# Two gates and the second modulation as row products on TensorE in four column groups, and one-column steps in VectorE's threshold search, in a decoder layer

## The chip, the cores and the metric

The kernel runs on one core of a Trainium2 chip. A core has five engines that run their own instruction streams and wait for each other by semaphores: TensorE (PE; its weight loads are listed as PEld), VectorE (DVE), ScalarE (ACT), GpSimd (POOL) and SyncE (SP), whose queue here issues nearly all DMA transfers. The metric is the device time of one execution in microseconds; lower is better.

## The reference

One decoder layer on x of 1024 tokens and 1024 channels in f32, conditioned by a vector c:

```
mod = silu(c) @ w_mod + b_mod        # 6 rows: shift1, scale1, gate1, shift2, scale2, gate2
h   = x * (1 + scale1) + shift1
q, k, v, u, iq, ik, iw = split(h @ w_in)
score = sum_h iw_h * relu(rope(iq)_h . rope(ik))      # causal
attn  = softmax attention of 8 heads over the 256 best keys by score
mix   = concat(attn, causal pooling of u over 2, 4, 8, 16 tokens) @ w_o
x = layer_norm(alpha * x + gate1 * mix)
h = x * (1 + scale2) + shift2
x = layer_norm(alpha * x + gate2 * ((silu(h @ w_gate) * (h @ w_up)) @ w_down))
```

Each row of mod is a product of the 1024 entries of silu(c) with a 1024 x 1024 block of w_mod (4 MB). The change concerns four of the six rows: gate1 (row 2), shift2 and scale2 (rows 3 and 4) and gate2 (row 5), in the change's own count rows 0 to 3.

## The kernel before, in words

The work stands in stages. First the first modulation and the index projections (to about 75 us). Then the score loop (to about 178 us): index logits on PE (`lg`), relu on ACT, weighted sums on DVE into `score`, for query tiles 2 to 7 of 128 tokens, with the Q projections (`pj`) between them. Then the projection (to about 374 us): 24 groups of 24 matmuls of 512 columns, eight for u (the pooling channels), eight for k and eight for v; their weights come by `raw_slot` transfers on SP's queue and are split into a rounded part (ACT) and a rest (POOL) in `ws_W`. After two groups of u, DVE adds shifted copies (`ub`), ACT and POOL split the result (`phi`, `plo`), and PE multiplies it with the pooling weights (`po`). Then the attention in head groups g = 3 to 0 (to about 545 us), the output product with w_o, a layer norm and the feed-forward part.

The 256 best keys of a query are found by a threshold search on 16-bit keys. DVE searches tiles 7 and 6 together (`colsD`, two columns, one for each tile) and tile 2 alone (`colsE`); ACT searches 5 and 4 together, and 3. `search_v` takes 31 steps a search: a counting pass over each tile's keys with the candidate as a scalar, and then two small operations that turn the counts `cntc` into the new candidate `cand`. The searches are fillers: a planner puts their steps wherever an engine would wait by its own estimates, and the programs of DVE, ACT and POOL are then fixed in the order in which they were written. An engine runs its instructions in that order.

In the score loop one step of `gate_acc` follows each part: a load of 512 KB and one DVE operation of 128 x 1024 that adds silu(c)[k] times the row block to `modacc`. `gate_fin`, at the projection's group 20, sums the partitions with two ones-matmuls (`gt`) and adds the bias. In the attention, from unit 8 on, `mods` runs two steps a unit: 16 DVE products with row sums over 128 x 1024 (`modraw`) for shift2 and scale2, and eight operations on `gacc` for gate2, which goes to `g2_d` by two more `gt`.

## Time and profile before

| | us |
|---|---|
| runs | 1322.65, 1324.58, 1326.92 (median 1324.58) |
| span of the profiled execution | 1321.4, mean granted TensorE clock 0.957 of full speed |
| own time of the profiled execution | not listed beside its span |
| busy in the span | PE 1199.6, PEld 934.3, DVE 1066.3, ACT 648.6, POOL 736.7 |

The profile shows one execution. Busy times of engines overlap, and a share over the whole span is a mean over stages with different limits, so the stages are read apart. The time outside the span (the 3.2 us between it and the median) is taken as it is.

### The profile page before, as it was taken

What the parts mean: (1) busy time and instruction counts of PE and PEld (TensorE: products, weight loads), DVE (VectorE), ACT (ScalarE), POOL (GpSimd) and SP (SyncE); (2) the same over time, 40 slices, a digit from 0 to 9 for tenths busy, and PEclk for the clock granted to TensorE, in tenths of its full rate; (3) what the DMA queues carried; (4) which work ended last, traced back from release to release, by engine and by line L of the source; (5) the groups of instructions that cost most, each with busy time, mean ns of one, the idle gap of its engine ahead of it and who ended that gap; (6) DMA issues with size and microseconds to landing.
All of it is one profiled execution on the core that took longest, in us unless ns stands there. A gap on an engine that the chain in (4) does not pass through costs nothing.

```text
span 1321.4 us, 16106 instructions
## 1 busy us (share of the span) xinstructions
PE 1199.6 (91%) x5462; PEld 934.3 (71%) x5462; DVE 1066.3 (81%) x1828; ACT 648.6 (49%) x1335; POOL 736.7 (56%) x509
## 2 busy tenths in 40 slices
PE   8979895797988996999789999999999999999996
PEld 6646564575855654787677787878788887878775
DVE  6899999999978797477697787776878777777698
ACT  3346673675998776445534243333333333333531
POOL 1392373666213355427678384664848475576848
PEclk8999898798979998999799999999999999999998
DMA  9540020131100266420020101102010111113112
GB/s 343 222 158 29 16 72 24 64 96 42 47 16 9 73 215 239 144 72 9 32 96 32 65 32 64 64 32 96 33 64 32 65 43 53 68 44 112 47 58 119
DMA packets 34904, 103.91 MB, mean 79 GB/s; under 512 B 3843, under 2 KB 3843, under 8 KB 33286
## 3 DMA queue, kind: packets, MB, share of 16 engines
q1 hardware_dynamic: 34822, 102.88, 22.1%
q8 instruction: 43, 0.70, 0.2%
q14 instruction: 39, 0.32, 0.1%
HBM read 93.42 MB, written 9.45 MB: 78 GB/s over the span
## 4 chain that ended last, share of the span: by engine, by line
PE 38%; DVE 6%; POOL 4%; issue 2%; ACT 1%; DVEq 0%; POOLq 0%; ACTq 0%
PE gu L169 24%; PE dn L169 14%; DVE act_W L169 2%; POOL wraw_R L169 1%; DVE utmp_X L169 1%; POOL wraw_W L169 1%; DVE gtmp_V L169 1%; POOL wblk_T L169 0%; DVE wblk_T L169 0%; DVE hr_H L169 0%; POOL hr_H L169 0%; DVE res_X L169 0%; DVE stat_C L169 0%; POOL wblk_V L169 0%; DVE wblk_V L169 0%
## 5 line engine op out<-in xcount | busy, mean ns | idle before, releaser
L169 PE MATMUL gu<-hr_H,wblk_T 128*128 128x512 f32 (+1 forms) x924 | 217.3, 387 | 3.0 <-POOL wblk_T L169 1.9
L169 PE MATMUL gu<-hr_H,wblk_V 128*128 128x512 f32 (+1 forms) x924 | 215.2, 384 | 3.7 <-POOL wblk_V L169 1.9
L169 PEld LDWEIGHTS gu<-hr_H,wblk_T 128*128 128x128 f32 x924 | 172.3, 191 | 39.2 <-POOL wblk_T L169 3.6
L169 PEld LDWEIGHTS gu<-hr_H,wblk_V 128*128 128x128 f32 x924 | 170.0, 188 | 40.1 <-POOL wblk_V L169 3.6
L169 DVE TENSOR_TENSOR res_X<-res_X,dn 128x512 f32<-128x512 f32 (+1 forms) x253 | 159.0, 678 | 15.4 <-PE dn L169 15.3
L169 POOL TENSOR_SCALAR sm_H<-sm_H,stat_X 128x1024 f32<-128x1024 f32 (+7 forms) x64 | 58.6, 928 | 124.1 <-DVE stat_X L169 112.5
L169 PE MATMUL pj<-ws_W,hT_H 128*128 128x512 f32 x456 | 119.4, 409 | 4.4 <-ACT pout_K L169 2.0
L169 POOL TENSOR_TENSOR wraw_R<-wraw_R 128x512 f32<-128x512 f32 x64 | 94.5, 1484 | 46.9 <-DVE wblk_T L169 23.7
L169 POOL TENSOR_TENSOR wraw_W<-wraw_W 128x512 f32<-128x512 f32 x60 | 86.7, 1452 | 58.0 <-DVE wblk_V L169 29.3
L169 PEld LDWEIGHTS pj<-ws_W,hT_H 128*128 128x128 f32 x456 | 85.1, 192 | 30.0 <-issue 10.1
L169 PE MATMUL dn<-wblk_T,act_W 128*128 128x512 f32 x324 | 79.6, 394 | 4.4 <-DVE act_W L169 4.4
L169 PE MATMUL dn<-wblk_V,act_W 128*128 128x512 f32 x324 | 78.5, 391 | 2.9 <-DVE act_W L169 2.5
L169 DVE TENSOR_SCALAR_CACHE_REDUCE junk_X<-keysD_T,colsD_X 128x1024 int16<-128x1024 int16 (+1 forms) x64 | 78.9, 1269 | 0.7
L169 ACT ACTIVATE wblk_V<-wraw_R 128x512 fp32r<-128x512 f32 x56 | 35.2, 629 | 80.7 <-POOL wraw_R L169 62.3
L169 PEld LDWEIGHTS dn<-wblk_T,act_W 128*128 128x128 f32 x324 | 60.9, 189 | 19.1 <-DVE act_W L169 6.5
L169 PEld LDWEIGHTS dn<-wblk_V,act_W 128*128 128x128 f32 x324 | 60.4, 188 | 17.4 <-DVE act_W L169 4.2
L169 POOL TENSOR_TENSOR ws_W<-raw_R,ws_W 128x1024 fp32r<-128x1024 f32 x17 | 44.8, 2652 | 48.6 <-ACT ws_W L169 48.5
L169 ACT ACTIVATE wblk_V<-wraw_W 128x512 fp32r<-128x512 f32 x53 | 33.1, 627 | 75.0 <-POOL wraw_W L169 56.4
L169 ACT ACTIVATE wblk_T<-wraw_W 128x512 fp32r<-128x512 f32 x56 | 35.0, 628 | 66.3 <-POOL wraw_W L169 50.2
L169 ACT ACTIVATE wblk_T<-wraw_R 128x512 fp32r<-128x512 f32 x52 | 32.5, 627 | 60.9 <-POOL wraw_R L169 45.5
L169 ACT ACTIVATE junkA_T<-keys_T,colsA_X 128x768 bf16<-128x768 uint16 (+3 forms) x62 | 54.1, 873 | 9.0 <-DVE colsA_X L169 8.7
L169 ACT ACTIVATE utmp_X<-gu 128x512 f32<-128x512 f32 x33 | 19.7, 598 | 73.4 <-PE gu L169 73.4
(300 smaller groups left out, 2828.1 us busy)
## 6 DMA issues: line engine op xcount, KB each, us to landing
wm_K<-in_wma_dram SPq DMA_DIRECT2D x16, 512.0 KB, 9.5
modraw_V<-in_wmc_dram SPq DMA_DIRECT2D x16, 512.0 KB, 4.5
wraw_R<-in_wg_dram SPq DMA_DIRECT2D x6, 1024.0 KB, 4.9
wraw_R<-in_wd_dram SPq DMA_DIRECT2D x12, 512.0 KB, 3.5
wraw_W<-in_wup_dram SPq DMA_DIRECT2D x12, 512.0 KB, 3.5
modraw_V<-in_wmg_dram SPq DMA_DIRECT2D x10, 512.0 KB, 4.3
wraw_R<-in_wup_dram SPq DMA_DIRECT2D x10, 512.0 KB, 3.5
wraw_W<-in_wg_dram SPq DMA_DIRECT2D x5, 1024.0 KB, 4.9
```

The costliest lines, as they stand in the source:

```text
L169: ins_ = f(*a, **k)
```

## The change

Both gates and the second modulation become row products on PE. The weights of the four rows come as 16 sets of 1 MB (`mset`, three slots in region K, where the score loop's operands were). A half (`mod_half`) is four plain-f32 matmuls with 32 columns of `silb` (32 copies of silu(c)[k]) stationary and 512 columns of the set moving; the four write to the four 32-partition groups of one PSUM bank `md`. Two halves make 512 columns of a row. ACT copies the bank with a scale of 1/32 (`macc`), and a ones-matmul sums the 128 partitions: for the gates as one full-width matmul (`gt`) with a 1 x 512 addition on DVE and a write to `gate_d`, for shift2 and scale2 as four products of one column (`mc`) with an addition of 128 x 4. This is done at the projection's groups 1 to 9, two halves a group. `gate_acc`, `gate_fin` and `mods` go away. The loads go through SP's queue, between the weight loads and behind the writes that stand there.

In `search_v` the two small operations on nt columns become nt operations of one column each, and the second is a TENSOR_SCALAR with the old candidate as a scalar operand, in place of a SCALAR_TENSOR_TENSOR with two tensor inputs.

```diff
@@ -45,7 +45,7 @@
-MODS = (8, 2)
+MOD_AT = 1
...
@@ -302,8 +304,6 @@
     srow = buf("X", 4224, 1024, "srow")
     SP.dma_start(srow, crow_in.to_broadcast([P, 1024]))
     A.activation(srow, srow, AF.Silu)
-    s_d = tc.dram_tile([1, 1024], F32, name="s_d")
-    SP.dma_start(s_d, srow[0:1, :])
@@ -427,93 +427,7 @@
...
-    def gate_acc(row, acc, ring, ahead):
...
-    def mods():
...
+    gate_d = [tc.dram_tile([1, 1024], F32, name=f"gate{q}_d") for q in range(2)]
...
@@ -680,9 +594,11 @@
                     dt = U16 if low else I16
                     V.tensor_scalar(trash(i).bitcast(dt), kv[i].bitcast(dt), one(cand, m), one(base, m),
                                     ALU.is_ge, ALU.add, accum_out=one(cntc, m))
-                V.tensor_scalar(pr, cntc, 0.0, float(1 << b), ALU.is_ge, ALU.mult)
                 off = -float(1 << (b - 1)) if b > 0 else -1.0
-                V.scalar_tensor_tensor(cand, pr, off, cand, ALU.add, ALU.add)
+                for m in range(nt):
+                    V.tensor_scalar(one(pr, m), one(cntc, m), 0.0, float(1 << b), ALU.is_ge, ALU.mult)
+                for m in range(nt):
+                    V.tensor_scalar(one(cand, m), one(pr, m), one(cand, m), off, ALU.add, ALU.add)
 
         def search_a(bits, low):
 
@@ -811,7 +727,6 @@
...
-            next(gate_steps, None)
...
@@ -893,13 +808,52 @@
     def v_take(t, pp):
         A.activation(vst[t // 4][:, t % 4], v3(pp), AF.Copy)
 
-    def gate_fin(dst, acc, row, base):
-        SP.dma_start(base, bg_in[row : row + 1, :].to_broadcast([P, 1024]))
-        for c in range(2):
+    MSET = [buf("K", 2048 + i * 2048, 2048, "mset") for i in range(3)]
+    silb = buf("X", 5312, 256, "silb")
+    grow = buf("X", 5568, 512, "grow")
+    macc = [buf("V", 5616 + i * 512, 512, "macc") for i in range(2)]
+    m_ps = {}
+
+    def mod_load(h):
+
+        if h < 16:
+            SP.dma_start(MSET[h % 3], wmr_in[h // 4, h // 2 % 2, h % 2])
+
+    def mod_half(h):
+
+        s_, part = divmod(h, 2)
+        if part == 0:
+            m_ps[s_] = psA("md")
+        for q in range(4):
+            k = 4 * part + q
+            T.matmul(m_ps[s_][32 * q : 32 * q + 32, :], silb[:, k * 32 : (k + 1) * 32], MSET[h % 3][:, q * 512 : (q + 1) * 512],
+                     start=(part == 0), stop=(part == 1))
+        mod_load(h + 3)
+        if part == 1:
+            A.activation(macc[s_ % 2], m_ps.pop(s_), AF.Copy, scale=1.0 / 32)
+
+    def mod_fin(s_):
+
+        row, c = divmod(s_, 2)
+        acc = macc[s_ % 2]
+        if row in (0, 3):
             pm = psA("gt")
-            cc = slice(c * 512, (c + 1) * 512)
-            T.matmul(pm, ones, acc[:, cc], start=True, stop=True)
-            V.tensor_tensor(dst[:, cc], base[:, cc], pm, ALU.add)
+            T.matmul(pm, ones, acc, start=True, stop=True)
+            V.tensor_tensor(grow[0:1, :], grow[0:1, :], pm[0:1, :], ALU.add)
+            SP.dma_start(gate_d[row // 3][:, c * 512 : (c + 1) * 512], grow[0:1, :])
+            if s_ != 7:
+                n = {0: 1, 1: 6, 6: 7}[s_]
+                SP.dma_start(grow[0:1, :], bg_in[n // 6 : n // 6 + 1, n % 2 * 512 : n % 2 * 512 + 512])
+        else:
+            pc = psA("mc")
+            for j in range(4):
+                T.matmul(pc[:, j : j + 1], acc[:, j * P : (j + 1) * P], ones[:, 0:1], start=True, stop=True)
+            u = (row - 1) * 8 + c * 4
+            V.tensor_tensor(m2[:, u : u + 4], pc[:, 0:4], bcol[:, 16 + u : 20 + u], ALU.add)
+            if s_ == 5:
+                V.scalar_tensor_tensor(h2c[:, 0:8], m2[:, 8:16], 1.0, lnc[:, 0:8], ALU.add, ALU.mult)
+                V.scalar_tensor_tensor(h2c[:, 8:16], m2[:, 8:16], 1.0, lnc[:, 8:16], ALU.add, ALU.mult)
+                V.tensor_tensor(h2c[:, 8:16], h2c[:, 8:16], m2[:, 0:8], ALU.add)
 
     def w_loads(w_in):
         for kp in range(3):
@@ -922,6 +876,11 @@
     while qt[2] or qt[0] < NT:
         q_piece()
     w_loads(wu_in)
+    for h in range(3):
+        mod_load(h)
+    SP.dma_start(lnc, lncol_in)
+    SP.dma_start(grow[0:1, :], bg_in[0:1, 0:512])
+    V.tensor_copy(silb.rearrange("p (k r) -> p k r", r=32), silc.unsqueeze(2).to_broadcast([P, 8, 32]))
     for i in range(4):
         G.memset(ub[i][:, 0:16], 0.0)
     for kp in range(4):
@@ -979,9 +938,17 @@
         else:
             at_(nd, lambda a=a, pp=pp: v_take(a, pp))
         if n_ == 20:
-            at_(n_, lambda: gate_fin(GR, macc, 0, raw_slot()))
+            SP.dma_start(GR, gate_d[0].to_broadcast([P, 1024]))
+        q_ = n_ - MOD_AT
+        if 0 <= q_ < 9:
+            if q_:
+                mod_fin(q_ - 1)
+            if q_ < 8:
+                mod_half(2 * q_)
         for f in late.pop(n_, []):
             f()
+        if 0 <= q_ < 8:
+            mod_half(2 * q_ + 1)
     last = len(groups)
     pinned.clear()
 
@@ -1151,11 +1118,6 @@
                     nrm += 1
             elif step == "T":
                 u_trans(u)
-        if n_ == MODS[0]:
-            mod_steps = mods()
-        if n_ >= MODS[0]:
-            for _ in range(MODS[1]):
-                next(mod_steps, None)
         if g > 0 and (pr, i % 2) in Q_AT:
             t = 2 * (g - 1) + 1 - Q_AT.index((pr, i % 2))
             q_make(t, q_load(t))
@@ -1168,8 +1130,6 @@
     while streams:
         advance(streams[0])
     times.fill = None
-    for _ in mod_steps:
-        pass
     wo_split(1)
     pair_cat(0, 3, pair_pv(0, 3))
     wo_split(2)
...
@@ -1861,8 +1821,7 @@
         "cnt": f(np.broadcast_to(cnt.reshape(1, 64), (P, 64))),
         "crow": f(a["c"][0].reshape(1, D)),
         "wma": f(np.stack([wmt[1], wmt[0]], axis=2).reshape(8, P, 2048)),
-        "wmc": f(wmt[3:5]),
-        "wmg": f(np.stack([wmod[:, :, 2], wmod[:, :, 5]]).reshape(2, 8, P, 1024)),
+        "wmr": f(np.stack([wmod[:, :, r] for r in (2, 3, 4, 5)]).reshape(4, 2, 4, P, 2, 512).transpose(0, 4, 1, 3, 2, 5).reshape(4, 2, 2, P, 2048)),
         "bcol": f(np.concatenate([np.stack([bmod[1].T, bmod[0].T], axis=2).reshape(P, 16), bmod[3].T, bmod[4].T], axis=1)),
         "bg": f(np.stack([bmod[2].reshape(-1), bmod[5].reshape(-1)])),
```

DVE's program, before, around the first `ub` addition of the projection (colsE is tile 2's search, colsD that of tiles 7 and 6):

```order
L169 TENSOR_SCALAR junk_X_614,colsE_X_616<-keysA_X_605,colsE_X_616 128x384
L169 TENSOR_SCALAR colsE_X_616<-colsE_X_616 128x1
L169 SCALAR_TENSOR_TENSOR colsE_X_616<-colsE_X_616 128x1
L169 TENSOR_SCALAR junk_X_614,colsE_X_616<-keysA_X_605,colsE_X_616 128x384
L169 SCALAR_TENSOR_TENSOR ub_V_1234<-ub_V_1234,ub_V_1232 128x1024
L169 TENSOR_SCALAR junk_X_607,colsD_X_615<-keysD_T_609,colsD_X_615 128x1024
```

The same place after (grow is the gate's row, gt its summed product):

```order
L171 TENSOR_TENSOR grow_X_1225<-grow_X_1225,gt_1435 1x512
L171 TENSOR_SCALAR junk_X_601,colsD_X_609<-keysD_T_603,colsD_X_609 128x1024
L171 TENSOR_SCALAR junk_X_602,colsD_X_609<-keysD_T_603,colsD_X_609 128x896
L171 TENSOR_SCALAR colsD_X_609<-colsD_X_609 128x1 x4
L171 TENSOR_SCALAR junk_X_601,colsD_X_609<-keysD_T_603,colsD_X_609 128x1024
L171 TENSOR_SCALAR junk_X_602,colsD_X_609<-keysD_T_603,colsD_X_609 128x896
L171 TENSOR_SCALAR colsD_X_609<-colsD_X_609 128x1 x4
L171 TENSOR_TENSOR grow_X_1225<-grow_X_1225,gt_1505 1x512
L171 SCALAR_TENSOR_TENSOR ub_V_1212<-ub_V_1212,ub_V_1210 128x1024
```

Tile 2's search stands wholly ahead of `ub` now (28 of its 31 steps did before, and 6 steps of colsD where 7 do now), and two gate additions stand ahead of it too.

PE's program, before, at the end of the fourth single u group and the first pooling product:

```order
L169 MATMUL pj_1519<-hT_H_67,ws_W_72 128x512 x3
L169 MATMUL pj_1519<-hT_H_68,ws_W_72 128x512 x3
L169 MATMUL po_1544<-phi_V_1236,wps_X_1231 128x512 x2
L169 MATMUL po_1544<-plo_V_1237,wps_X_1231 128x512
```

PE's program after, from the third row product to the next group (md_1522's second row needs the sixth set):

```order
L171 MATMUL pj_1480<-hT_H_68,ws_W_72 128x512 x3
L171 MATMUL gt_1505<-macc_V_1227,const_C_78 128x512
L171 MATMUL md_1522<-mset_K_1222,silb_X_1224 32x512 x4
L171 MATMUL md_1522<-mset_K_1223,silb_X_1224 32x512 x4
L171 MATMUL pj_1556<-hT_H_61,ws_W_69 128x512 x3
```

Two more groups, two more md pairs and the `mc` of each stand between this and the first `po`, which was the next thing behind the u groups before.

SP's queue, before, from the last piece of wu (in_wu) on:

```order
L166 DMA q_d<-rope_V_454 128x512 x5
L166 DMA raw_R_75<-in_wu_dram 128x1024
L166 DMA raw_R_73<-in_wpool_dram 128x512
L166 DMA raw_R_74<-in_wk_dram 128x1024
L166 DMA raw_R_75<-in_wk_dram 128x1024
L166 DMA q_d<-rope_V_454 128x512
```

SP's queue after, from the same place:

```order
L168 DMA q_d<-rope_V_450 128x512 x5
L168 DMA mset_K_1221<-in_wmr_dram 128x2048
L168 DMA q_d<-rope_V_450 128x512
L168 DMA mset_K_1222<-in_wmr_dram 128x2048
L168 DMA mset_K_1223<-in_wmr_dram 128x2048
L168 DMA raw_R_75<-in_wu_dram 128x1024
...
L168 DMA mset_K_1221<-in_wmr_dram 128x2048
L168 DMA q_d<-rope_V_450 128x512
L168 DMA mset_K_1222<-in_wmr_dram 128x2048
L168 DMA gate_d<-grow_X_1225 1x512
L168 DMA mset_K_1223<-in_wmr_dram 128x2048
```

Three sets stand ahead of the last piece of wu, and the sixth set stands behind the gate's first write, which waits for DVE.

## Rows read from the trace of the kernel before

**Rows 1.** Busy time of each engine in stretches of the span (us, with the number of instructions), then the granted TensorE clock as a share of full speed, the DMA engines' busy share and what they moved: score loop, projection, and three parts of the attention.

```profile
74.00:178.00 104.00, 92.25 (x357) 58.40 (x357) 100.42 (x162) 66.29 (x116) 49.91 (x34) 0.92 0.12 44
178.00:374.00 196.00, 156.46 (x649) 124.20 (x647) 189.43 (x360) 129.92 (x346) 101.88 (x65) 0.90 0.18 59
374.00:442.00 68.00, 60.27 (x311) 37.44 (x312) 45.88 (x94) 60.25 (x143) 19.77 (x18) 0.87 0.04 14
442.00:516.00 74.00, 62.14 (x384) 38.92 (x383) 67.68 (x155) 49.04 (x116) 35.95 (x32) 0.95 0.57 196
516.00:545.00 29.00, 27.79 (x173) 19.31 (x172) 15.94 (x56) 20.72 (x60) 14.56 (x19) 1.00 0.44 155
```

**Rows 2.** What PE waited for in the projection (178 to 374 us): us in total, times, the longest.

```profile
PE po L169 <- ACT ub_V L169: 15.1, 1, 15.1
PE pair L169 <- POOL ws_W L169: 12.2, 4, 4.3
PE kT L169 <- DVE kr_K L169: 5.1, 2, 4.8
PE po L169 <- POOL plo_V L169: 2.5, 2, 1.7
PE pj L169 <- ACT pout_K L169: 2.0, 1, 2.0
PE po L169 <- ACT phi_V L169: 1.3, 1, 1.3
```

**Rows 3.** The timeline (start, duration, instruction; in brackets the idle time before it and its releaser): PE at the end of the score loop and at the first group, PE and DVE at the first pooling product, DVE and PE at the start of the attention.

```profile
171.83 7.09 PE L169 MATMUL pj<-ws_W,hT_H 128*128 128x512 f32 x30
181.26 0.98 PE L169 MATMUL pair<-hT_H,ws_W 128*128 128x512 f32 x3 [1.88 <-POOL ws_W L169]
...
211.81 1.97 PE L169 MATMUL pj<-hT_H,ws_W 128*128 128x512 f32 x8
226.03 1.22 DVE L169 SCALAR_TENSOR_TENSOR ub_V<-ub_V,ub_V 128x1024 f32<-128x1024 f32 x1
228.88 1.22 PE L169 MATMUL po<-phi_V,wps_X 128*128 128x512 f32 x2 [15.09 <-ACT ub_V L169]
...
373.17 0.63 DVE L169 TENSOR_SCALAR score_X<-junk_X 128x896 f32<-128x896 bf16 x1
374.46 0.73 PE L169 MATMUL s<-kr_K,qab_H 128*128 128x512 f32 x2 [1.90 <-ACT qab_H L169]
```

**Rows 4.** DVE's instructions that the change takes away: the first gate in the score loop (groups of one tile, busy us and mean ns behind the bar; the first with its least, median and greatest ns), the second modulation and gate in the attention, and the second gate's additions.

```profile
L169 DVE TENSOR_SCALAR modacc_X<-modraw_T,const_C x1: 1774/1774/1774, 75.6 to 75.6; 128x1024 f32<-128x1024 f32 x1
L169 DVE SCALAR_TENSOR_TENSOR modacc_X<-modraw_T,const_C,modacc_X 128x1024 f32<-128x1024 f32 x3 | 5.9, 1956 | 0.0
L169 DVE SCALAR_TENSOR_TENSOR modacc_X<-modraw_V,const_C,modacc_X 128x1024 f32<-128x1024 f32 x2 | 3.6, 1787 | 0.0
L169 DVE SCALAR_TENSOR_TENSOR modacc_X<-modraw_X,const_C,modacc_X 128x1024 f32<-128x1024 f32 x2 | 3.4, 1698 | 0.0
...
L169 DVE CUSTOM_DVE_ANT_0 modraw_V<-modraw_V,srow_V 128x1024 f32<-128x1024 f32 x16 | 20.3, 1266 | 0.6 <-DMA modraw_V<-in_wmc_dram 0.6
L169 DVE SCALAR_TENSOR_TENSOR gacc_V<-modraw_V,const_C,gacc_V 128x1024 f32<-128x1024 f32 x7 | 10.0, 1431 | 0.0
L169 DVE TENSOR_SCALAR gacc_V<-modraw_V,const_C x1: 740/740/740, 494.2 to 494.2; 128x1024 f32<-128x1024 f32 x1
L169 DVE TENSOR_TENSOR grow_V<-grow_V,gt x2: 670/673/676, 513.7 to 515.4; 1x512 f32<-1x512 f32 x2
```

**Rows 5.** The search's small operations on DVE, 74 to 375 us: busy us and mean ns behind the bar.

```profile
L169 DVE SCALAR_TENSOR_TENSOR colsD_X<-colsD_X 128x2 f32<-128x2 f32 x31 | 18.4, 592 | 0.7
L169 DVE TENSOR_SCALAR colsD_X<-colsD_X 128x2 f32<-128x2 f32 x33 | 18.0, 546 | 0.8
L169 DVE SCALAR_TENSOR_TENSOR colsE_X<-colsE_X 128x1 f32<-128x1 f32 x31 | 11.5, 371 | 0.6
```

**Rows 6.** The timeline of DVE and POOL at three search steps: beside POOL's pooling sums, beside its weight split, and with POOL idle.

```profile
229.55 0.15 DVE L169 TENSOR_SCALAR colsE_X<-colsE_X 128x1 f32<-128x1 f32 x1
229.67 1.13 DVE L169 TENSOR_SCALAR colsD_X<-colsD_X 128x2 f32<-128x2 f32 x1
...
253.08 4.67 POOL L169 TENSOR_TENSOR ws_W<-raw_R,ws_W 128x1024 fp32r<-128x1024 f32 x2
253.41 2.03 DVE L169 TENSOR_SCALAR colsD_X<-colsD_X 128x2 f32<-128x2 f32 x1
255.48 2.28 DVE L169 SCALAR_TENSOR_TENSOR colsD_X<-colsD_X 128x2 f32<-128x2 f32 x1
...
271.77 0.17 DVE L169 TENSOR_SCALAR colsD_X<-colsD_X 128x2 f32<-128x2 f32 x1
271.97 0.16 DVE L169 SCALAR_TENSOR_TENSOR colsD_X<-colsD_X 128x2 f32<-128x2 f32 x1
```

**Rows 7.** The timeline of PE: the first gate's two ones-matmuls (plain f32, two records each), and the attention's products o with two 64-column groups (two records each) between transposes pT.

```profile
353.45 1.88 PE L169 MATMUL gt<-modacc_X,const_C 128*128 128x512 f32 x4
354.76 1.02 PE L169 MATMUL pj<-ws_W,hT_H 128*128 128x512 f32 x2
...
402.62 0.38 PE L169 MATMUL o<-pT_H,vf_V 128*64 128x256 f32 x1
402.94 0.55 PE L169 MATMUL pT<-const_C,sm_H 128*128 128x128 f32 x3
403.41 3.45 PE L169 MATMUL o<-pT_H,vf_V 128*64 128x256 f32 x30
406.80 1.47 PE L169 MATMUL pT<-const_C,sm_H 128*128 128x128 f32 x11
```

**Rows 8.** Transfers: the feed-forward part's loads of 1 MB (count, KB each, median us from issue to landing), what the DMA engines moved in the first 50 us (last column, GB/s), and ACT's wait for the last piece of wu.

```profile
wraw_R<-in_wg_dram SPq DMA_DIRECT2D x6, 1024.0 KB, 4.9
0.00:50.00 50.00, 42.80 (x194) 34.05 (x195) 36.73 (x60) 15.16 (x15) 7.76 (x11) 0.93 0.90 342
184.82 1.06 ACT L169 ACTIVATE ws_W<-raw_R 128x1024 fp32r<-128x1024 f32 x1 [2.80 <-DMA raw_R<-in_wu_dram]
```

**Rows 9.** PE in the attention: what score matmuls waited for from 374 to 442 us, and the timeline around the second gate's product.

```profile
PE s L169 <- DVE stat_X L169: 5.2, 7, 1.4
...
507.38 0.82 PE L169 MATMUL s<-kr_K,qab_X 128*128 128x256 f32 x4 [3.74 <-DVE stat_X L169]
511.60 3.75 PE L169 MATMUL gt<-gacc_V,const_C 128*128 128x512 f32 x4 [3.41 <-DVE stat_X L169]
```

More of the change, by code (lines that the diff above doesn't have):

```diff
@@ L136, in __init__, with cost @@
         self.tc, self.eng, self.name, self.pinned, self.times, self.t = tc, eng, name, pinned, times, 0.0
-    def cost(self, op, out, k):
-        n = 1
+    def cost(self, op, aps, k):
+        out, n = aps[0], 1
         for s_ in out.shape[1:]:
@@ L171, in call @@
                 at = max(self.t, tm.ready(self.name, outs, ins))
-                self.t = at + self.cost(op, aps[0], k)
+                self.t = at + self.cost(op, aps, k)
                 tm.done(self.name, outs, ins, self.t)
@@ L184, in decoder_layer_kernel @@
     tc: tile.TileContext,
[L185 removed]
+    x_in, xT_in, c_in, cs_in, cnt_in, crow_in, wma_in, wmr_in, bcol_in, bg_in,
     wiq_in, wikw_in, wu_in, wq_in, wk_in, wv_in, wpool_in, pscale_in, wo_in,
@@ L428, in decoder_layer_kernel @@
     psq[7] = pp7
-    macc = buf("X", 5504, 1024, "modacc")
-    MRING = [buf("T", 0, 1024, "modraw"), buf("T", 1024, 1024, "modraw"), buf("X", 6528, 1024, "modraw"),
-             buf("V", 7168, 1024, "modraw")]
-    n_m = [0]
-    def mring():
-        n_m[0] += 1
-        return MRING[n_m[0] % 4]
-    def gate_acc(row, acc, ring, ahead):
-        slots = []
-        def load(k):
-            if k < KT:
-                wm = ring()
-                SP.dma_start(wm, wmg_in[row, k])
-                slots.append(wm)
-        for k in range(ahead):
-            load(k)
-        for k in range(KT):
-            load(k + ahead)
-            if k == 0:
-                V.tensor_scalar(acc, slots[k], silc[:, 0:1], None, ALU.mult)
-            else:
-                V.scalar_tensor_tensor(acc, slots[k], silc[:, k : k + 1], acc, ALU.mult, ALU.add)
-            yield
@@ L894, in v_take @@
         A.activation(vst[t // 4][:, t % 4], v3(pp), AF.Copy)
-    def gate_fin(dst, acc, row, base):
-        SP.dma_start(base, bg_in[row : row + 1, :].to_broadcast([P, 1024]))
-        for c in range(2):
-            pm = psA("gt")
-            cc = slice(c * 512, (c + 1) * 512)
-            T.matmul(pm, ones, acc[:, cc], start=True, stop=True)
-            V.tensor_tensor(dst[:, cc], base[:, cc], pm, ALU.add)
+    MSET = [buf("K", 2048 + i * 2048, 2048, "mset") for i in range(3)]
+    silb = buf("X", 5312, 256, "silb")
@@ L1724, in decoder_layer_kernel @@
             if not mults:
-                SP.dma_start(GR, g2_d.to_broadcast([P, 1024]))
+                SP.dma_start(GR, gate_d[1].to_broadcast([P, 1024]))
         for e in ADDS[n]:
```

53 lines of the change are left out of this document (4 added, 49 removed).

## The prediction

> **What bounds the kernel now.** The change touches the score loop, the projection and the attention, so I cut the profile by these stages first [rows 1]; behind the attention, from some 545 us on, the instructions stay what they were. In the score loop (74 to 178 us) DVE is busy 100.4 of 104 us and PE 92.3; in the projection (178 to 374 us) DVE 189.4 of 196 us and PE 156.5. So DVE sets the pace up to the attention, and PE follows with 11.7 and 39.5 us of idle time. In the attention the picture turns: in its first part (374 to 442 us) PE and ACT are busy 60.3 and 60.3 of 68 us and DVE only 45.9; in the part in which the second modulation runs (442 to 516 us) DVE is back at 67.7 of 74; the rest, to 545 us, has PE at 27.8 of 29.
>
> Next I asked what PE waits for in the projection [rows 2]: 15.1 us for ub, 12.2 us for split weights from POOL, 5.1 us for kr, 5.8 us in small ones, 38.2 us in all. The 15.1 us are one wait, at the pooling matmul po: PE's last matmuls before it start at 211.8 us, DVE's ub add only at 226.0 us, po at 228.9 us [rows 3]. DVE was not waiting itself: it had search steps in front of the add. At the start of the attention both are late together: DVE's last search operation begins at 373.2 us, the first score matmul at 374.5 us [rows 3].
>
> **What leaves VectorE.** The gate operations in the score loop are one of 1.77 us, three of 5.9 in sum, two of 3.6 and two of 3.4 [rows 4]: 14.6 us. In the attention 16 products of the second modulation take 20.3 us and the second gate's eight operations 10.0 + 0.7 [rows 4]: 31.0 us.
>
> The search edit is worth more than it looks. The two-column steps take 592 and 546 ns on average, the one-column second step 371 ns [rows 5]. Standing alone, the two-column ones take 0.17 and 0.16 us; while POOL splits weights from 253.08 to 257.75 us in two operations, the same two take 2.03 and 2.28 us, and each ends as one of POOL's two does [rows 6]. A one-column TENSOR_SCALAR takes 0.15 us right in front of a two-column one of 1.13 us [rows 6]. So the long ones seem to stand still while POOL works, and the new form does not. The excess is 31 x (0.43 + 0.38) + 31 x 0.21 = 31.6 us. The four new one-column operations issue close behind each other; I add 0.1 us a step, 3 us. With the first gate's two old additions gone (taken at 0.7 us each, as the second gate's grow additions [rows 4]) and the new ones come (four of 0.67 us, four on 4 columns, one copy: about 4 us), DVE has some 41 us less to do before the attention. Alone it could be through by 333 us; so PE sets the start of the attention afterwards, and DVE's gain is not the kernel's.
>
> **What comes to TensorE.** 64 plain-f32 matmuls, 32 columns stationary and 512 moving. One full-width matmul of this kind is two records of 0.43 us: four records begin at 353.45 us and the next group at 354.76 us, with 1.88 us of modelled busy time [rows 7]; 0.86 us each. How four column groups overlap, no row shows; two do: 30 records of 64 stationary and 256 moving columns take 3.45 us [rows 7], 0.115 us each, where half of 0.43 would be 0.215. So two groups run twice as fast. Bounds for the 64: 55 us without overlap, 27.5 us at two, 13.8 us at four. I take four, plus 2 us for changing between shapes, 16 us (1.0 us for a half of four matmuls): the switch from o to pT and back at 402.62, 402.94 and 403.41 us costs 0.2 us at most [rows 7], and there are about 32 switches, so 0 to 6 us. The Trainium skill, "TensorE: Matmul & The Clock Gate", Part 3, gives 2.38 times for three such groups; at that share of the ideal the 64 would take 17 us. "TensorEngine Tiling (Array Packing)", Key Properties, speaks against the change: it says that changing the tiling mode drains TensorE. The switch at 402.62 us shows no more than the 0.2 us, so by the one the sum has 6 us more than with none, and I hold it at 2. Then four ones-matmuls of 0.86 us where there were four (two of them move here from the attention), and 16 one-column products at the 0.13 us of pT [rows 7], 0.5 us for each four. ACT gets eight copies of 0.6 us; it is busy 129.9 of 196 us here [rows 1], which hides them, and without that cover they cost 5 us.
>
> **The transfers.** The bytes are the same, 16 MB, but now 16 loads of 1 MB between the other loads of SP's queue. Such a load lands after 4.9 us [rows 8]; at the 342 GB/s of the first 50 us [rows 8] one takes 3.1 us of the engines, two 6.1 us, and a group with its two halves and its gate product takes 5.5 + 2.0 + 0.5 = 8 us. (A group is 24 matmuls; 30 take 7.09 us with the last one's tail [rows 3], so 24 some 5.5.) It fits with little to spare. Two places are late. The fourth piece of wu now follows three sets in the queue; before, nothing of that size was ahead of it, and ACT had it at 184.82 us after a wait of 2.8 us [rows 8]. I charge 4 us, where 3 MB ahead of it could cost 9. And the sixth set stands behind the write of gate_d, which waits for DVE's first grow addition. That addition comes two steps before ub. To ub DVE has by its order one [7,6] step, three [2] steps with the search's tail and the additions more, and the gate and the excess of 6 and 28 steps less: 226.0 - 14.6 - 4.9 - 5.9 + 2.9 + 1.9 + 3.4 + 1.6 = 210.4 us. So the addition is done at 203.9 us and the sixth set lands at 208.8.
>
> **The sum.** (1) PE can win at most its 11.7 us of idle in the score loop; I take 8: projection from 170.8 us. (2) Up to the second half of the third row product: four groups 22, six halves 6, two gate products 1.7, the late wu 4: 204.5 us; the set comes at 208.8. Then a half, two groups, two times mc, three halves: 16 us, po at 224.8 instead of 228.9 us, 4 earlier, and ub is no longer late. (3) From po to the attention there were 145.6 us. Add seven halves, two gate products and two mc, less the two old ones, 8 us; of the remaining 21.2 us of waits (38.2 less po's 15.1 and the 1.9 of the first group [rows 3]) I keep 6, since DVE is ahead and POOL has more time for each group's weights. That is 7 us less: attention from 363.5 us, 11 earlier. (4) In the attention, the score matmul at 507.38 us waits 3.74 us for DVE, the gate product 3.41 us, and its own work is 3.75 us [rows 9]: 10.9 us. Of the 5.2 us that score matmuls wait for stat before 442 us [rows 9] I take half. 13.5 us. (5) Behind it nothing. Together 24.5 us: a span of 1296.9 us instead of 1321.4. The profiled span is 3.2 us under the median of the runs, 1324.58; I carry that over: **1300 us**.
>
> **Rivals.**
> *The column groups do not overlap* (the other side). Then the 64 cost 55 instead of 16 us; of the 39 the stall at the sixth set takes up 4. The gain of 24.5 becomes a loss of 10.5: 1335 us. It decides from about 0.7 us a matmul. For it: nothing here shows four groups. Against it: two overlap fully.
> *The sets come late each time.* If the two loads of a group took their 4.9 us one after the other, a group would last 9.8 instead of 8 us, over eight groups 14 us more: 1314 us.
> *The attention gives nothing back.* ACT is busy 60.3 of 68 us in its first part [rows 1] and may be next: 13.5 us less gain, 1314 us.
> *The one-column steps stand still like the old ones* (the change doesn't do what it says). Then ub and the first grow addition come 11 us later, the sixth set at 220 us, po at 236, and DVE has only 10 us less to do before the attention, which starts no earlier than now; with 13.5 us from the attention, 1311 us. Against it: the 0.15 us beside POOL.
> *More is won.* No stall at the sixth set or at wu (8 us), all waits of (3) gone (6), all of PE's idle time in the attention between 374 and 516 us, 19.6 us, less what I took (some 8 more): 1278 us.
>
> **How the numbers follow.** Forecast 0.50 (1290 to 1309 us); more won 0.14; attention gives nothing 0.12; standing still 0.06; late sets with other losses that eat the gain 0.08, most of it within the bound of no change; no overlap, or transfers that stall every group, 0.10. About 0.3%, 4 us, is what a measurement can tell here: the three runs lie within 4.3 us. Faster 0.83, same 0.06, slower 0.11. The range of 8 in 10 runs from half of the better case to the edge of no change: 1275 to 1320 us.
>
> **What would show it.** Right: md records at some 0.1 us pitch; the two-column steps gone and no step of the search over 0.3 us; DVE idle before the attention, PE the engine that is waited for; PE's wait at po gone, with a smaller one for a set in its place; the first score matmul near 363 us; no DVE wait around the end of the second modulation's old place. Wrong: md records at 0.43 us; PE waits for mset several times; a score matmul that starts at 363 us but an attention as long as before, with ACT's waits in front of it.

## The result, and the profile after

The changed kernel takes 1308.64 us (median of four runs, 1307.53 to 1309.66); the kernel before, run beside it, 1323.9. The ratio is 0.9885 [0.9863, 0.9907]: faster by 1.15%, 15 us. The forecast was 1300, its range 1275 to 1320. The profiled span is 1307.9 us where the sum gave 1296.9, so 13.5 of the 24.5 us came.

The same stretches as [rows 1], after (busy us of PE, its weight loads, DVE, ACT and POOL, granted clock, DMA share, GB/s):

```profile
74.00:178.00 104.00, 90.58 (x361) 57.59 (x360) 86.45 (x182) 65.28 (x115) 43.70 (x33) 0.94 0.10 36
178.00:374.00 196.00, 177.61 (x826) 129.32 (x824) 166.08 (x403) 131.65 (x334) 100.29 (x66) 0.95 0.36 131
374.00:442.00 68.00, 58.22 (x287) 36.23 (x285) 44.28 (x85) 59.54 (x149) 18.62 (x16) 0.85 0.04 11
442.00:516.00 74.00, 70.72 (x487) 47.95 (x489) 50.64 (x151) 63.26 (x162) 37.19 (x44) 0.98 0.25 83
```

In the projection the engines have changed places: PE has 177.6 of 196 us to do (before 156.5), DVE 166.1 (before 189.4). What PE waited for there, as in [rows 2]:

```profile
PE gt L171 <- ACT macc_V L171: 9.9, 1, 9.9
PE pair L171 <- POOL ws_W L171: 2.5, 2, 2.3
PE md L171 <- DMA mset_K<-in_wmr_dram: 2.5, 1, 2.5
PE gt L171 <- DVE grow_X L171: 1.8, 1, 1.8
```

The 15.1 us at po are gone, and with 16.7 us against 38.2 PE stands less; but 9.9 us are a new wait, for the copy of a row product. And po still comes 19 us later than before. The timeline of PE, DVE, ACT, POOL and SP's queue, in order of time, answers [rows 3] and [rows 7]:

```profile
79.86 2.34 POOL L171 TENSOR_TENSOR ws_W<-raw_R,ws_W 128x1024 fp32r<-128x1024 f32 x1
82.26 4.64 PE L171 MATMUL pj<-ws_W,hT_H 128*128 128x512 f32 x11 [5.11 <-POOL ws_W L171]
...
181.34 0.61 PE L171 MATMUL pair<-hT_H,ws_W 128*128 128x512 f32 x2
...
204.05 0.69 DVE L171 TENSOR_TENSOR wps_X<-raw_R,wps_X 128x512 fp32r<-128x512 f32 x1
212.09 0.60 ACT L171 ACTIVATE macc_V<-md 128x512 f32<-128x512 f32 x1 [12.94 <-DMA q_d<-rope_V]
212.74 2.08 PE L171 MATMUL gt<-macc_V,const_C 128*128 128x512 f32 x2 [9.93 <-ACT macc_V L171]
213.74 8.83 POOL L171 TENSOR_TENSOR ub_V<-ub_V 128x1024 f32<-128x1024 f32 x4 [14.01 <-ACT ub_V L171]
215.88 1.94 DVE L171 TENSOR_SCALAR keysA_X<-score_X,colsE_X 128x384 bf16<-128x384 f32 x1
218.57 1.81 DVE L171 TENSOR_TENSOR_SCAN score_X<-keysA_X,colsE_X 128x384 bf16<-128x384 bf16 x1
220.42 2.27 DVE L171 TENSOR_SCALAR score_X<-score_X 128x384 bf16<-128x384 bf16 x1
223.91 0.68 DVE L171 TENSOR_TENSOR grow_X<-grow_X,gt 1x512 f32<-1x512 f32 x1
224.95 0.34 SPq L168 DMA_DIRECT2D mset_K<-in_wmr_dram  x1
229.78 1.93 PE L171 MATMUL md<-mset_K,silb_X 128*32 128x512 f32 x8 [2.49 <-DMA mset_K<-in_wmr_dram]
230.75 1.21 DVE L171 SCALAR_TENSOR_TENSOR ub_V<-ub_V,ub_V 128x1024 f32<-128x1024 f32 x1
...
238.71 1.92 PE L171 MATMUL md<-mset_K,silb_X 128*32 128x512 f32 x16
247.03 1.07 PE L171 MATMUL md<-mset_K,silb_X 128*32 128x512 f32 x8
248.03 0.73 PE L171 MATMUL po<-phi_V,wps_X 128*128 128x512 f32 x2
...
373.66 2.79 PE L171 MATMUL s<-kr_K,qab_H 128*128 128x512 f32 x8 [1.57 <-ACT qab_H L171]
```

Read it from ub upwards. DVE reaches ub at 230.75 us; the forecast had 210.4. Ahead of it stand the two grow additions, two steps of tiles 7 and 6 between them, and the tail of tile 2's search (214.15 to 223.9 us; its three largest operations are shown). The first addition is done at 224.6 us instead of 203.9, so the sixth set is issued at 224.95 and used at 229.78 (forecast 208.8). The wait that was not on the list is ACT's 12.94 us: macc lies where the rope buffer was, and its last write to q_d stands in SP's queue behind a wk load that waits for DVE's wps at 204.05. This wait makes a second limit for ub: ACT copies the u products for POOL only behind macc, so POOL's sums, which ub needs, run from 213.74 to 222.57 us. However free DVE had been, ub could not have started before that.

The stages laid beside the sum, from these rows (`pair` is the projection's first group, `s` the score matmuls of the attention), [rows 3] and the first gate-and-up product of the feed-forward part (637.24 us before, 622.37 after):

| us | before | forecast | after |
|---|---|---|---|
| projection's first pair starts | 178.8 | 170.8 | 181.3 |
| pair to po | 50.1 | 54.0 | 66.7 |
| po to first s | 145.6 | 138.6 | 125.6 |
| first s to feed-forward | 262.8 | 249.3 | 248.7 |
| feed-forward to the end | 684.2 | 684.2 | 685.5 |

Against the forecast 10.5 us were lost at the start and 12.7 up to po, and 13.0 came back behind po.

### The profile page after: what moved, and what is told of

Its sections match the earlier page's. It is cut to its first block, busy times and chain, and to the rows that moved or that the text cites. A ratio compares the mean times of both kernels' runs of the same rounds, so it can differ in the third digit from the quotient of the medians.

```text
span 1307.9 us, 16418 instructions
## 1 busy us (share of the span) xinstructions
PE 1211.9 (93%) x5622; PEld 936.8 (72%) x5622; DVE 1001.6 (77%) x1846; ACT 650.4 (50%) x1343; POOL 718.7 (55%) x509
## 4 chain that ended last, share of the span: by engine, by line
PE 55%; DVE 24%; ACT 7%; POOL 6%; issue 6%; DMA 1%; SPq 0%; DVEq 0%; POOLq 0%; ACTq 0%
PE gu L171 24%; PE dn L171 14%; DVE junk_X L171 4%; PE wo L171 4%; DVE score_X L171 4%; PE pj L171 3%; PE s L171 2%; DVE act_W L171 2%; PE pair L171 2%; PE pT L171 2%; PE o L171 2%; POOL wraw_R L171 2%; DVE stat_C L171 1%; DVE utmp_X L171 1%; DVE hr_H L171 1%
## 5 line engine op out<-in xcount | busy, mean ns | idle before, releaser
L171 DVE TENSOR_TENSOR res_X<-res_X,dn 128x512 f32<-128x512 f32 (+1 forms) x253 | 159.0, 678 | 15.4 <-PE dn L171 15.3
L171 POOL TENSOR_TENSOR wraw_R<-wraw_R 128x512 f32<-128x512 f32 x64 | 94.7, 1487 | 47.0 <-DVE wblk_T L171 23.7
L171 POOL TENSOR_SCALAR sm_H<-sm_H,stat_X 128x1024 f32<-128x1024 f32 (+7 forms) x64 | 49.7, 791 | 116.7 <-DVE stat_X L171 106.1
L171 PEld LDWEIGHTS dn<-wblk_V,act_W 128*128 128x128 f32 x324 | 60.4, 188 | 17.4 <-DVE act_W L171 4.2
L171 ACT ACTIVATE wblk_V<-wraw_W 128x512 fp32r<-128x512 f32 x53 | 33.1, 627 | 75.0 <-POOL wraw_W L171 56.4
```

What stands on the lines that cost most here:

```text
L171: ins_ = f(*a, **k)
```

## The experiments

"Kernel after" is the changed one. All ratios are to the kernel before, run beside each.

**Which half of the change pays.** e3_search is the kernel before with nothing but the new `search_v`; e4_rows is the kernel after with the old one, `V.scalar_tensor_tensor` on two columns.

> The kernel before with the one-column search steps alone (both gates and the second modulation as before). Theory A: the excess of 31.6 us in the two-column and two-input steps goes away, less some 3 us for the added operations; DVE, which sets the pace to the attention, is through some 28 us earlier, and PE, which waits 38 us in the projection, follows in part: attention 15 to 25 us earlier, 1300 to 1310 us. Rival B: the waiting moves to other DVE operations beside POOL, or PE is next at once: 1318 to 1324 us.

> The changed kernel with the old two-column search steps. Theory A: DVE has some 28 us more to do before the attention than in the changed kernel, where its search ended 10 us before the first score matmul; attention 15 to 20 us later, 1322 to 1328 us, so that the row products alone gain nothing. Rival B: PE sets the pace with its row products, and the time stays within 5 us of the changed kernel's 1308.6 us.

e3_search: 1310.48 us, 0.9908 [0.9871, 0.9944]. e4_rows: 1319.38 us, 0.9984 [0.9967, 1.0002]. The projection in e3_search, and then in e4_rows:

```profile
178.00:374.00 196.00, 168.00 (x683) 130.85 (x682) 177.40 (x440) 147.24 (x383) 103.40 (x67) 0.89 0.18 60
```
```profile
178.00:374.00 196.00, 171.85 (x790) 124.91 (x790) 186.54 (x342) 125.91 (x316) 100.36 (x67) 0.94 0.36 132
```

The search edit alone gives 11 us: first s at 359.1 instead of 374.5 us. The row products alone give nothing that can be told from no change: DVE is nearly as full as before (186.5 us), its search ends behind 374 us, the first s comes at 384.4, ten later; the attention is 17 us shorter, and 4 us go behind it. Together the two give 15 us, but that this is more than the search edit alone is not shown: the intervals of the two ratios overlap (0.9863 to 0.9907 and 0.9871 to 0.9944). The stages say why. Against e3_search, the kernel after has its first s 14.6 us later (373.7 us), and an attention that is 15.5 us shorter (248.7 us from the first s to the feed-forward part, 264.2 in e3_search): what the row products save there they cost ahead of it. The change also holds a new price for plain-f32 matmuls in the planner's estimates, by which the fillers are placed; e4_rows has it, e3_search has not, and no run varies it alone.

**Do the column groups overlap?** e8_one_group puts the four matmuls of a half into one column group, the first half in group 0 and the second in group 1, so that the sums behind them go over 64 partitions:

```diff
-            T.matmul(m_ps[s_][32 * q : 32 * q + 32, :], silb[:, k * 32 : (k + 1) * 32], MSET[h % 3][:, q * 512 : (q + 1) * 512],
-                     start=(part == 0), stop=(part == 1))
+            T.matmul(m_ps[s_][32 * part : 32 * part + 32, :], silb[:, k * 32 : (k + 1) * 32], MSET[h % 3][:, q * 512 : (q + 1) * 512],
+                     start=(q == 0), stop=(q == 3))
...
-            A.activation(macc[s_ % 2], m_ps.pop(s_), AF.Copy, scale=1.0 / 32)
+            A.activation(macc[s_ % 2][0:64], m_ps.pop(s_)[0:64], AF.Copy, scale=1.0 / 32)
...
```

> The changed kernel with the four matmuls of a half in one and the same 32-column group (first half in group 0, second in group 1; the sums behind them over 64 partitions), so that nothing can overlap within a half. It prices the rival of the prediction in which column groups do not overlap. Theory A: a half takes 3.4 us in place of 1.0, 16 halves 39 us more, of which PE's stops in the first groups (14 us) take up some 10: 1335 to 1340 us. Rival B: matmuls in one column group overlap as well, or most of the 39 us is hidden: under 1320 us.

1330.67 us, 1.0077 [1.0061, 1.0094], some 4 us under what was expected. A half:

```profile
251.20 3.62 PE L171 MATMUL md<-mset_K,silb_X 128*32 128x512 f32 x8
```

The eight records take 3.62 us where the kernel after has 1.07, both with the tail of the last one. In after, 16 records take 1.92 us, 0.12 each, two to a matmul: 0.24 us, and 15.4 us for the 64 at this pitch (forecast 16). The overlap is worth 22 us of the kernel's time (25 by the two ratios), and without it the change is slower than before: the rival on the other side was rightly placed, at 1335. No drain can be seen between md and its neighbours: in the kernel after the half at 247.03 us ends, by its 1.07 us, at 248.10, and po begins at 248.03.

**The late start.** Dropping `s_d`, a 4 KB write, lets the scheduler order the first 100 us in another way: POOL's third split of the Q weights comes at 79.86 us instead of 71.81, five instructions later on POOL; PE waits 5.11 us for it, and the first lg moves from 78.2 to 86.7 us. e2_order puts the write back, unused.

> The changed kernel with one unused 4 KB write of silu(c) to DRAM kept, as the kernel before has it; with it the early instructions stand in the order of the kernel before (POOL's third split of the Q weights five instructions earlier). Theory A: the first index logits start at 78 us in place of 86.7 us, DVE gets its first score work 7 us earlier and all that follows to the attention moves by some 8 us: 1300 us. Rival B: the delay is taken up in the score loop or at PE's later waits, 1306 to 1309 us.

1306.93 us, 0.9882 [0.9847, 0.9918]: first lg at 77.4, but po at 244.9 and first s at 370.6. Of 9.3 us won at the start 3 are left at the attention, and the time cannot be told from that of the kernel after. Something behind the start soaks them up.

**Is it the macc copy?** e1_slot moves macc's first slot by 4 KB within the same buffer; e6_act takes the first gate and the columns out of PSUM on ACT, not DVE, with macc in another buffer (one slot, not two), the low part of wps on POOL and the biases added later; e7_act_order is e6_act with `s_d`.

```diff
-    macc = [buf("V", 5616 + i * 512, 512, "macc") for i in range(2)]
+    macc = [buf("V", 6640 - i * 1024, 512, "macc") for i in range(2)]
```
```diff
-    macc = [buf("V", 5616 + i * 512, 512, "macc") for i in range(2)]
+    macc = [buf("X", 5824, 512, "macc")] * 2
...
+                A.activation(grow[0:1, :], pm[0:1, :], AF.Copy)
...
-            V.tensor_tensor(m2[:, u : u + 4], pc[:, 0:4], bcol[:, 16 + u : 20 + u], ALU.add)
+            A.activation(m2[:, u : u + 4], pc[:, 0:4], AF.Copy)
```

> The changed kernel with the two macc slots laid on other parts of the rope buffer, so that ACT's first copy of a row product no longer waits for the last write of q_d (12.9 us of ACT and 9.9 us of PE in the changed kernel's profile). Theory A: that wait is PE's loss, and the attention starts 8 to 10 us earlier, 1300 us. Rival B: the sixth set waits for DVE's first grow addition (224.5 us in the changed kernel's profile) whatever ACT does, so PE stands still at the sixth set in place of the gate product and the time stays at 1307 to 1309 us.

> The changed kernel with every link from the row products' chain back to DVE cut in the projection's first groups: the gate-1 row and the shift2 and scale2 columns are taken out of PSUM by ACT (their biases are added later, by DVE, at group 20), the macc buffer lies outside the rope buffer, and the low part of the pooling weights is made on POOL, so that the third k load no longer stands before the fourth set waiting for DVE. Theory A: PE's three stops before the first po (9.9, 1.8 and 2.5 us in the changed kernel) go away; po then waits for ub alone (DVE at 230 us) and comes at 233 to 236 in place of 248 us; from po on PE is busy without a break, so the attention starts some 9 to 12 us earlier: 1297 to 1300 us. Rival B: DVE's search, which ended 10 us before the first score matmul, or ACT's searches are the limit just behind, and the gain is under 4 us: 1305 to 1309 us.

> The same with the unused 4 KB write of silu(c) kept, so that the early instructions stand in the order of the kernel before. Theory A: 3 us less again, as the write alone brought with the chain in place; 1294 to 1297 us. If DVE's early start now reaches po undamped, up to 8 us less: 1290 us. Rival B: as in the run beside it, within 1 us of that.

e1_slot: 1309.33 us, 0.9912 [0.9879, 0.9944]. It decides nothing, since the first copy still waited for all writes to q_d (17.4 us). e6_act: 1313.30, 0.9943 [0.9924, 0.9961]; e7_act_order: 1308.99, 0.9914 [0.9898, 0.993]. Both missed what was hoped for, and e6_act lies above its rival's 1309 too, with the first s at 377.3 us. PE's largest waits in e6_act, and its ub:

```profile
PE mc L171 <- ACT macc_X L171: 11.5, 1, 11.5
PE pair L171 <- POOL ws_W L171: 4.3, 2, 3.6
```
```profile
228.66 1.22 DVE L171 SCALAR_TENSOR_TENSOR ub_V<-ub_V,ub_V 128x1024 f32<-128x1024 f32 x1
```

The wait for macc at gt is gone, and PE stands as long at the next product: ACT's third macc copy is queued behind phi, and phi waits for ub, which has hardly moved. POOL's sums now end at 214.5 us, 14 us ahead of ub, so nothing but DVE's queue can hold it here. The stop belongs to ub.

**An earlier ub, first try.** In e9_hold no search step of tiles 7 and 6 is put between wps and ub; e10_hold_order adds `s_d`; e11_hold_late, with `s_d` too, holds them back only from behind wps on.

```diff
         V.scalar_tensor_tensor(cur[:, 16:PADW], cur[:, 16:PADW], 1.0 / WINDOWS[g], own[:, 16:PADW], ALU.mult, ALU.subtract)
+        times.fill = fill
...
+    times.fill = None
     split(wps, wp_raw[:, 0:512], 512)
```

> One edit against the kernel after: from the split of the pooling weights (wps) up to the first addition of ub, no search step is put among VectorE's instructions. So VectorE does the rest of the search of tile 2, then wps, the two grow additions and ub, one right behind the other, and all steps of tiles 7 and 6 come after ub (10 of their instruction groups stood ahead of it, about 30 us of VectorE). Theory (VectorE's place for ub is the wall of this stretch, and ScalarE's late macc copies and the late sixth set follow from the late wps and the late grow): wps at about 185 to 192 instead of 204.05, the third wk load and the q_d write behind it 12 to 18 us earlier, so ScalarE's wait for q_d (12.9 us) and TensorE's for macc (9.9 us) are gone or under 3 us; ub at 210 to 218 instead of 230.75, now bound by GpSimd's sums; po at 230 to 236 instead of 248.0; po to the attention 126 to 132 us as in the runs before, first s at 358 to 366 instead of 373.66; the search, which loses up to 12 us of VectorE's time ahead of ub, ends at 363 to 372. Time 1295 to 1303 against 1308.6 of the kernel after (ratio to the kernel before 0.981 to 0.987). Rival 1 (TensorE's own work bounds the stretch to the attention, the stops are cover for nothing else): po comes earlier, po to s grows by as much, time 1306 to 1310. Rival 2 (the search becomes the bound once its steps are moved behind ub): search end at 376 or later, first s not before 372, time 1308 to 1316.

> The edit of e9 together with the unused 4 KB write of s_d that restores the order of the kernel before in the first 100 us. Theory: first lg at 77 to 78 instead of 86.7; as before only about 3 us of these 9 reach the attention, since ub is bound by GpSimd's sums, which follow TensorE's u products: if the wall at ub is gone, more of the early gain comes through, 3 to 8 us: po at 222 to 232, first s at 352 to 362, time 1288 to 1300. Rival 1 (TensorE's work is the bound from here on): the early 9 us come through in full, since TensorE starts the projection earlier, 1290 to 1298, with po to s above 135. Rival 2 (search is the bound): the search end decides, 1300 to 1310.

> As e10, but steps of tiles 7 and 6 are still put in ahead of wps; only from wps to the first ub are there none. Theory: wps at about 195 (as in e2), ub at 207 to 214 where e2 had 227.5; ScalarE's wait for q_d stays at 8 to 12 us, so TensorE's stop at gt stays, about 8 us; po at 232 to 238 where e2 had 244.9; first s at 360 to 366 (e2 370.6); time 1297 to 1303 (e2 1306.9). It tells how much of a gain of e10 is due to ub and grow, and how much to the earlier wps and the q_d write behind it. Rivals as for e10.

e9_hold: 1321.01 us, 0.9994 [0.9977, 1.0012]; e10_hold_order: 1317.60, 0.9967 [0.9952, 0.9981]; e11_hold_late: 1310.79, 0.9916 [0.9883, 0.9949]. None came to the time that its theory gave. The second rival had the mechanism, the search as the bound, but its times were too low as well. DVE and PE in e9_hold:

```profile
212.19 0.68 DVE L171 TENSOR_TENSOR grow_X<-grow_X,gt 1x512 f32<-1x512 f32 x1 [10.17 <-PE gt L171]
221.93 1.21 DVE L171 SCALAR_TENSOR_TENSOR ub_V<-ub_V,ub_V 128x1024 f32<-128x1024 f32 x1
240.23 0.73 PE L171 MATMUL po<-phi_V,wps_X 128*128 128x512 f32 x2 [1.30 <-DVE const_C L171]
365.21 1.35 PE L171 MATMUL s<-kr_K,qab_H 128*128 128x512 f32 x4 [1.59 <-ACT qab_H L171]
379.78 0.63 DVE L171 TENSOR_SCALAR score_X<-junk_X 128x896 f32<-128x896 bf16 x1
381.18 1.94 PE L171 MATMUL s<-kr_K,qab_H 64*128 64x512 f32 x4 [14.62 <-DVE qab_H L171]
```

ub, po and the first s come 8.8, 7.8 and 8.5 us earlier, one for one, as expected, though ub not at 210 to 218: wps comes at 201.34 us, not by 192, since tile 2's search still stands ahead of it. And DVE idles for gt (10.17 us here, 23.0 in all), the search of tiles 7 and 6 ends at 380.4 instead of 363.7 us, and PE then waits 14.62 us for the operand queued behind it. e11_hold_late has to be laid beside e2_order, which has `s_d` as well: its first s comes 4 us earlier (366.6 us), its search ends 13 later (373.3), and its time is no better. An early ub and an early search of tiles 7 and 6 both need DVE's time; tile 2's search, which still stands ahead of both, serves neither.

**An earlier ub, second try.** Tile 2's mask is first used late in the attention. Its steps are written last, but not kept in that place as the other searches' are (I had taken the written order to hold for all), and the scheduler draws them forward: 32 counting passes and a tail ahead of ub. e12_tile2 keeps them in their place; e13_tile2_order adds `s_d`.

```diff
         q = queues[st[1][0]]
+        if st[3] == LATE:
+            pinned.add("V")
         try:
...
+        if st[3] == LATE:
+            pinned.clear()
```

> One edit against the kernel after: the search steps of tile 2 are pinned to the place at which the program writes them, behind the search of tiles 7 and 6, as those of the other tiles are; in the kernel after they are free, and the scheduler draws them forward in front of wps, grow and ub. Tile 2's mask is first used late in the attention. So e9 and e11 are mended at their fault: ub comes early, and no step of tiles 7 and 6 is put off for it. Theory (what stands in front of ub on VectorE is the wall; e9 showed that an earlier ub brings po and the first s forward one for one, as long as the search of tiles 7 and 6 is done by then): the projection a little earlier or at the same 181, wps at 188 to 197 instead of 204.05, ScalarE's wait for q_d gone or under 5 us, ub at 211 to 218 instead of 230.75, po at 229 to 236 instead of 248.0, po to s 125 to 131, first s at 356 to 365 instead of 373.66, the search of tiles 7 and 6 at its end by 335 to 352; the attention, which now holds some 20 to 30 us of tile 2's steps on VectorE (108 us busy of 171 there), gets longer by 0 to 5 us. Time 1291 to 1303 against 1308.6. Rival 1 (the steps of tile 2 cost in the attention what they free ahead of it): first s earlier, but the attention longer by 10 us and more, 1306 to 1313. Rival 2 (TensorE's own work bounds the stretch from the projection to the attention): po earlier, po to s at 138 or more, 1304 to 1309.

> The edit of e12 together with the unused 4 KB write of s_d, which restores the order of the first 100 us. Theory: first lg at 77 to 78, the projection 3 to 5 us earlier than in e12; with nothing of tile 2 ahead of ub the early gain is no longer damped at ub: first s 3 to 6 us earlier than in e12, time 1286 to 1299, about 4 us below e12. Rival 1 (GpSimd's sums or the wait of macc for q_d hold the stretch, not VectorE): as e12 to within 1 us. Rival 2 (the steps of tile 2 cost the attention what they free): 1304 to 1311.

e12_tile2: **1295.38 us, 0.9791 [0.9774, 0.9808]**. e13_tile2_order: **1286.38 us, 0.9727 [0.9712, 0.9741]**, the fastest of all, 22 us below the kernel after (21 by the two ratios). The timeline of e12_tile2, and what PE waited for there from its first s to the feed-forward part:

```profile
171.53 0.61 PE L171 MATMUL pair<-hT_H,ws_W 128*128 128x512 f32 x2
...
198.00 0.68 DVE L171 TENSOR_TENSOR grow_X<-grow_X,gt 1x512 f32<-1x512 f32 x1 [2.01 <-PE gt L171]
207.03 1.21 DVE L171 SCALAR_TENSOR_TENSOR ub_V<-ub_V,ub_V 128x1024 f32<-128x1024 f32 x1
223.95 0.73 PE L171 MATMUL po<-phi_V,wps_X 128*128 128x512 f32 x2
...
337.41 0.63 DVE L171 TENSOR_SCALAR score_X<-junk_X 128x896 f32<-128x896 bf16 x1
347.98 1.35 PE L171 MATMUL s<-kr_K,qab_H 128*128 128x512 f32 x4 [1.58 <-ACT qab_H L171]
```
```profile
PE s L171 <- DVE colsE_X L171: 4.0, 4, 1.4
PE s L171 <- DVE qab_H L171: 3.7, 1, 3.7
```

ub comes 23.7 us earlier than in after, po 24.1, the first s 25.7; PE's wait for macc before gt is down to 1.2 us. Two things were not in the expectation: the score loop ends 9 us earlier too (last lg group at 162.9 instead of 172.3 us), as tile 2's steps no longer stand between its sums; and the attention gives back 9.8 us (258.5 instead of 248.7 from the first s to the feed-forward part), of which the two waits above are 7.7; 2 us more go behind it. The earlier end of the score loop is 9.8 us of the 23.7 at ub (first pair at 171.53 instead of 181.34). POOL's sums end at 206.1 us and ub follows at 207.03, so DVE's queue no longer holds it back. In e13_tile2_order the early start comes through in full:

```profile
196.78 1.21 DVE L171 SCALAR_TENSOR_TENSOR ub_V<-ub_V,ub_V 128x1024 f32<-128x1024 f32 x1
213.70 0.73 PE L171 MATMUL po<-phi_V,wps_X 128*128 128x512 f32 x2
337.69 1.36 PE L171 MATMUL s<-kr_K,qab_H 128*128 128x512 f32 x4 [1.57 <-ACT qab_H L171]
```

Each is 10.2 or 10.3 us ahead of e12_tile2, and the kernel 9.0 us: where ub held, the same edit had brought 3 us at the attention. No run keeps tile 2 in its place in the kernel before, which also has most of tile 2's search ahead of ub; so what the row products are worth beside this edit stays open.

## Why the prediction was right, and where its steps were not

That the time fell 9 us from the forecast is in part luck: the sum lost 23.2 us up to po and got 13.0 back behind it, mostly from the clock, which it had not priced.

**Right: the sign, the size of the product and the attention.** The md price held (15.4 us for 16), the four mc products take 0.95 us (I had 0.5), and the attention wins 14.1 us (I had 13.5). Of the latter the second gate's product and waits are gone (the score matmul that waited 3.74 us waits 0.35), but the 2.6 us from the other stat waits did not come: from 374 to 442 us they are 5.7 us after, 5.2 before; what gave the rest is not traced. DVE's two-column steps no longer stand still, but less came of it than worked out from [rows 5]: with the one-column first step (5.2 us) these rows are 53.1 us before and 33.1 after, 20 us less where the 31.6 less 3 were counted, since the one-column operations cost more than the 0.1 us a step that I added. What is left of them, after:

```profile
L171 DVE TENSOR_SCALAR colsD_X<-colsD_X 128x1 f32<-128x1 f32 x128 | 16.7, 178 | 0.0
L171 DVE TENSOR_SCALAR colsE_X<-colsE_X 128x1 f32<-128x1 f32 x66 | 11.7, 178 | 1.3
L171 DVE TENSOR_SCALAR colsD_X<-colsD_X 128x2 f32<-128x2 f32 x2 | 4.7, 2328 | 0.0
```

The one-column steps take 178 ns on average, 217 at most, beside POOL too; the two operations still on two columns took 2.33 us each. "PE sets the start of the attention afterwards" was right as well: DVE is through at 363.7 us, ten before the first s.

**Step (1), failed.** The projection was to start at 170.8; it started at 181.3. The loop itself became 6 us shorter (93.3 to 87.4 us from the first to the last lg, forecast 8), but it began 8.5 later. That dropping the write moves unrelated instructions stands in the order of the two programs on POOL, which I had not compared for that stretch; e2_order shows the cause.

**Step (2), the one that cost most.** Its mechanism was right, with the sixth set behind gate_d, gate_d behind the first grow addition, and the addition behind DVE's queue. Its size was not: the addition was to be done at 203.9 us and was at 224.6. The largest term is the first gate's 14.6 us, which the sum took off in full. In the kernel after they are idle time: DVE is busy 100.4 of the score loop's 104 us before and 86.5 after. Without the late start (e2_order) DVE is busy 97.0 us there, yet the addition begins only 3.3 us earlier (220.66); where the rest goes stays open. The tail of tile 2's search was charged at 2 to 3 us and took about 10. The six steps of [7,6] ahead of ub had 0.7 us of excess to lose where I counted 4.9: before, only one of their operations was long (0.85 us at 194.90). And a path was missing: the wait of macc for q_d, which holds POOL's sums to 222.57 us and so by itself put ub at 210.4 out of reach; e6_act shows that without it PE stops elsewhere for the same ub. e12_tile2 shows what the step should have asked: not only how long what stands ahead of ub takes, but whether it has to stand there.

**Step (3), better than forecast.** po to s took 125.6 us, not 138.6. Of the 13.0 us, 3.7 are waits (I kept 6 us where 2.3 were left). Nearly all the rest goes with the clock, which I had left out. Two stretches before, behind PE's 15.1 us stop, and around its waits for plo (1.7 us) and for weights (4.3 us):

```profile
229.00:236.00 7.00, 6.27 (x14) 4.46 (x15) 7.00 (x14) 6.97 (x20) 6.84 (x4) 0.51 0.09 36
250.00:260.00 10.00, 5.70 (x14) 3.98 (x14) 9.89 (x9) 4.79 (x11) 7.59 (x5) 0.51 0.29 79
```

and the like stretch after, with PE busy throughout:

```profile
250.00:260.00 10.00, 10.00 (x57) 6.38 (x58) 6.92 (x23) 8.24 (x19) 6.37 (x4) 1.00 0.72 261
```

In the two stretches with stops the clock is at its lower level (1.2 GHz, 0.51 granted), in the one without at the upper (2.4 GHz, 1.00). From po to s the mean went from 0.91 to 0.99, and PE's busy time stayed (122.6 and 121.7 us) although 8 us of work had been added. So these waits on PE cost more than their own length.

**The rivals.** No overlap: priced well by e8_one_group, and false. Late sets: a load of 1 MB lands after 6.0 us at the median, but PE waited for a set once, 2.5 us, and because of the grow addition. "The attention gives nothing back" is false. "One-column steps stand still" is false by the 178 ns. "More is won" (1278) did not come; e13_tile2_order gets to 1286 by another road.

## What to carry to other kernels

On an engine that runs in order, the time of an instruction that others wait for is set by what is queued ahead of it; list those predecessors, and ask of each when its result is first needed. A filler with a late use ahead of a product with many waiters costs more than a long wait seen elsewhere, and cutting the visible wait only moves it to the next link (e6_act). Compare the order of all engines over the whole program, also where the change does nothing: a dropped 4 KB write cost 9 us at the start, of which 3 reached the attention in one kernel (e2_order) and 10 in another (e13_tile2_order). And before bringing an instruction forward, look at what is put off for it (e9_hold).
